# Halving the on-chip scratch of dynamic DMAs and giving the room to four more buffer slots

## The chip, the cores and the metric

The kernel runs on one core of a Trainium2 chip, as one program launched once. The metric is the device time of that launch in microseconds (us). The core has a matrix engine (TensorE, PE in the profile, with its weight loads shown as PEld), a vector engine (VectorE, DVE), a scalar engine (ScalarE, ACT), a general engine (GpSimd, POOL) and a queue engine that only issues transfers (SyncE, SP). Each works through its own queue of instructions in order, and they wait for each other by semaphores. TensorE's clock has two levels, 1.2 and 2.4 GHz; the profile gives the granted clock of a stretch as a share of the higher one.

## The reference, cut to what matters

Two transformer-like blocks of two layers each run one after the other on one sequence of 512 tokens with 1024 channels, in float32.

```python
def first_block(x, c, ...):
    h = layer_norm(x)
    for l in range(2):
        ada = (silu(c) @ w_ada[l] + b_ada[l])           # six modulation vectors
        u = h * (1.0 + sc1) + sh1
        y = mixer(u, ...)        # bidirectional mLSTM + dilated attention, gated, projected
        h = layer_norm(DN_ALPHA * h + g1 * y, ...)
        u = h * (1.0 + sc2) + sh2
        h = layer_norm(DN_ALPHA * h + g2 * swiglu(u, w1[l], w3[l], w2[l]), ...)
    return h

def second_block(x, c, ...):
    for layer in range(2):
        sh1, sc1, g1, sh2, sc2, g2 = adaln_params(c, ada_w[layer], ada_b[layer])
        h = rms_norm(x, ...) * (1.0 + sc1) + sh1
        if layer == 0:           # RG-LRU branch and stick-breaking attention
            mix = concat([lru(...) * gelu(gr), stick_breaking(q, k, v)]) @ ev_w_out
        else:                    # sliding-window attention with sinks
            mix = swa_sinks(q, k, v, sinks) @ od_w_out
        x = x + g1 * mix
        h = rms_norm(x, ...) * (1.0 + sc2) + sh2
        x = x + g2 * conv_ffn(h, ...)
    return x
```

Stick-breaking attention takes, per head and block of 128 queries, the scores `z`, `sp = softplus(z)` where the key is earlier than the query, the reversed running sum of `sp`, and the weights `exp(z - sum)`, which multiply the values.

## The kernel before, in words

Activations lie with channels on the 128 partitions and the 512 tokens along the row: a `[1024, 512]` array is eight tiles of 128 x 512 float32, 2048 bytes of a partition each. Every such tile, and every half of a high/low pair, is one **slot**. The pool has `NSLOT` of them (line 30). `Model.get` (line 561) takes the slot at the head of a queue `freeq`, and `Model.put` (line 566) hands slots back at its tail, so slots go round first in, first out; with F slots free, a `get` returns the slot that was handed back F `put`s earlier, and its first writer has to wait until the last reader of its former content is through. This is settled when the program is built. The framework then orders the instructions of each queue, sets the waits and lays out the memory: the scratch of the dynamic DMAs first, then constants, two buffers `wt` for raw weights, five pairs `wh`, `wl` for split weights, and the slots at the end.

Precision comes from splitting: a float32 value is a rounded part (high) and a remainder (low), and a projection sums three products. Weights arrive as one stream of 128 x 128 blocks, 16 to a transfer of 1 MB on SP's queue (line 596); for each eight of them ACT makes the high part (line 601) and DVE the low part (line 604). `proj` (lines 616 to 618) does three matmuls for each of the eight blocks into one of three `acc` banks of PSUM. PSUM further has two score banks `s` (pool `pss`), one bank `t` for transposes (`pst`) and two banks `o` (`pso`).

The stages, in order, with the lines that matter here:

- The start: `x` is loaded, normed (`Norm.plain`), and the first modulation is made tile by tile (`ada_tile`, line 830): four loads into slots (line 837, SP), matmuls (line 841), a copy (line 845), a transpose by matmul (line 848), a sum (line 850, DVE); then `u` (lines 1381 to 1383) and the first projections (lines 1388 to 1390).
- For each of two layers of the first block: four mLSTM heads, four attention pairs (`attention_pair`), gates and output projections (`mixer`), then the feed-forward (`ffn_first`). At the end of a pair POOL writes row sums to DRAM (line 1210) and reads them back spread over partitions with four DMAs (line 1214); DVE takes their difference (line 1218), ACT its tanh (line 1219). The next projections' gates are evacuated on ACT at line 1249. Inside a pair DVE writes the masked scores into a slot at line 1159, and the weighted values are summed by matmuls at lines 1189 and 1193.
- The joint between the blocks (`Chain`) norms twice at once, in two halves of 256 tokens: matmuls of squares and cross products (line 469), evacuations (line 487 on ACT, 488 on DVE), statistics, then the outputs tile by tile (lines 512 to 516, of which line 515 is on ACT). Line 665 is the first projection that reads them.
- The second block's first layer (`mix_even`, line 1608): the LRU, whose small weights come by DMAs on ACT's queue into a slot `bd` (line 1517), then four pairs of heads of stick-breaking attention (`stick_weights`, line 1567). For each pair the four query blocks run from the last to the first; the next pair's queries, keys and values (`heads`, with the head's norm at line 1447) are made after the first block. A step for one query block does for both heads: scores (lines 1487, 1488, 1576), two evacuations into slots `z` (line 1579) and `e` (line 1580), exponential and logarithm (1581, 1582), `sp` (1583), running sum (1584), difference (1586), exponential (1587), transposes (1590), evacuation (1591); then the weighted values (line 1604). `z` and `sp` go back after the transposes, `e` after the weighted values.
- The feed-forward, the sliding-window layer (`mix_odd`) and the last feed-forward.

Of the kernel before, what the change touches and what calls it, by code (L numbers as in the profile page):

```python
# [26 lines left out]
NBLK = 4176  # L27
CHUNK = 16
NCHUNK = NBLK // CHUNK
NSLOT = 57  # L30


FULL, HALF, MOVING = 0, 16, 112
# [493 lines left out]
class Model:  # L527
    def __init__(self, ctx, tc, ins, out, dbg=None, stop=None):
# [13 lines left out]
        self.slots = pool("slots", 1)  # L542
        self.freeq = deque(range(NSLOT))
        self.peak = NSLOT
        self.late = []
# [1307 lines left out]
```

## Time and profile before

| | us |
|---|---|
| median of 3 runs (3498.55 to 3499.63) | 3498.85 |
| the profiled execution's own time | 3499.55 |
| its span, first to last instruction | 3497.8 |
| PE busy in it | 3398.8 (97%) |
| DVE busy | 2158.0 (62%) |
| ACT busy | 1454.3 (42%) |
| POOL busy | 186.1 (5%) |
| mean granted clock of TensorE | 0.987 |

The profile records one execution. Busy time of an engine is the union of its instructions; the ends of matmuls are modelled, since they are pipelined. In a list of waits, "X L1 <- Y L2: a, n, b" says that engine X stood idle before its instruction of line 1 for a us in n waits, the longest b us, and that each ended when the instruction of line 2 on Y was done. In a timeline a line gives the start, the length, the engine, the line of the kernel, the operation, what it writes and reads, and in brackets the idle time of the engine before it and what ended that. A "q" behind an engine's name means its queue: a transfer that is issued there.

### The profile page before, as it was taken

How to read it: one execution, taken by the hardware profiler on the slowest of the kernel's cores; microseconds unless marked ns; L12 is line 12 of the kernel's file. 1: busy time of each engine (PE TensorE's matmuls, PEld its weight loads, DVE VectorE, ACT ScalarE, POOL GpSimd, SP SyncE). 2: the span in 40 equal slices, each digit the busy share in tenths (PEclk: the TensorE clock that was granted, in tenths of full speed). 3: DMA queues.
4: the chain of work that ended last, by engine and by line, in shares of the span. 5: the costliest groups of instructions: out<-in, count | busy, mean ns of one | idle time of the engine just before them, and what ended most of it. 6: DMA issues, size and time to landing. Idle time of an engine off the chain costs nothing.

```text
span 3497.8 us, 45346 instructions
## 1 busy us (share of the span) xinstructions
PE 3398.8 (97%) x17783; PEld 2791.3 (80%) x17783; DVE 2158.0 (62%) x4071; ACT 1454.3 (42%) x2536; POOL 186.1 (5%) x257
## 2 busy tenths in 40 slices
PE   7999998999999999999999999989999999999999
PEld 5888776878888888877688888877688888888887
DVE  5875544658664687555534856368788565875353
ACT  4543554224222554345423422237753233754231
POOL 1110011010000011001101000001000000000000
PEclk9999999999999999999999999999999999999999
DMA  5222222544552222222222546221136442113221
GB/s 217 91 79 79 84 73 79 206 156 164 187 209 103 76 88 79 91 73 73 86 90 85 186 176 210 99 70 61 37 108 220 162 148 86 60 61 109 96 97 73
DMA packets 76117, 395.72 MB, mean 113 GB/s; under 512 B 9200, under 2 KB 10480, under 8 KB 42496
## 3 DMA queue, kind: packets, MB, share of 16 engines
q1 hardware_dynamic: 69408, 377.90, 30.4%
q0 software_dynamic: 4480, 12.69, 1.2%
q8 instruction: 140, 2.29, 0.3%
q10 hardware_dynamic: 2016, 2.25, 0.2%
q14 instruction: 73, 0.60, 0.1%
HBM read 390.60 MB, written 2.20 MB: 112 GB/s over the span
## 4 chain that ended last, share of the span: by engine, by line
PE 44%; DVE 4%; ACT 1%; issue 1%; DMA 0%; DVEq 0%; ACTq 0%
PE acc L616 12%; PE acc L618 12%; PE acc L617 11%; PE acc L665 1%; PE acc L669 1%; PE acc L668 1%; PE o L1604 1%; PE t L1707 0%; DVE wl L604 0%; PE s L1487 0%; DVE slot L1584 0%; PE o L665 0%; PE o L668 0%; PE o L669 0%; PE s L1488 0%
## 5 line engine op out<-in xcount | busy, mean ns | idle before, releaser
L616 PE MATMUL acc<-slot,wh 128*128 128x512 f32 x3461 | 1368.5, 395 | 31.1 <-ACT slot L1249 14.3
L617 PE MATMUL acc<-slot,wh 128*128 128x512 f32 x3461 | 1363.1, 394 | 1.2 <-DVE slot L697 1.2
L618 PE MATMUL acc<-slot,wl 128*128 128x512 f32 x3461 | 1359.1, 393 | 0.0
L601 ACT CAST wh<-wt 128x1024 fp32r<-128x1024 f32 x522 | 547.7, 1050 | 1204.5 <-PE acc L617 1002.2
L604 DVE TENSOR_TENSOR wl<-wt,wh 128x1024 fp32r<-128x1024 f32 x522 | 645.5, 1238 | 512.3 <-ACT wh L601 504.0
L616 PEld LDWEIGHTS acc<-slot,wh 128*128 128x128 f32 x3461 | 654.1, 189 | 179.5 <-ACT slot L1249 15.1
L617 PEld LDWEIGHTS acc<-slot,wh 128*128 128x128 f32 x3461 | 653.9, 189 | 138.2 <-issue 6.0
L618 PEld LDWEIGHTS acc<-slot,wl 128*128 128x128 f32 x3461 | 653.3, 189 | 136.8 <-issue 5.0
L800 DVE SCALAR_TENSOR_TENSOR slot<-wada,csil,slot 128x512 f32<-128x512 f32 x308 | 231.8, 753 | 69.8 <-DMA wada<-in_ada_dram 64.1
L665 PE MATMUL acc<-slot,wh 128*128 128x256 f32 x726 | 206.9, 287 | 6.8 <-ACT slot L515 6.0
L668 PE MATMUL acc<-slot,wh 128*128 128x256 f32 x726 | 205.1, 283 | 0.0
L669 PE MATMUL acc<-slot,wl 128*128 128x256 f32 x726 | 204.1, 282 | 0.1
L696 ACT CAST slot<-slot 128x512 fp32r<-128x512 f32 x204 | 124.8, 619 | 174.6 <-POOL slot L1268 51.9
L1287 DVE SCALAR_TENSOR_TENSOR slot<-acc,ada,slot 128x512 f32<-128x512 f32 (+1 forms) x109 | 70.1, 646 | 155.4 <-PE acc L618 117.9
L895 DVE SCALAR_TENSOR_TENSOR slot<-acc,vecs,slot 128x510 f32<-128x510 f32 (+2 forms) x217 | 159.8, 745 | 7.6 <-ACT slot L890 4.9
L697 DVE TENSOR_TENSOR slot<-slot,slot 128x512 fp32r<-128x512 f32 x204 | 138.7, 688 | 24.6 <-ACT slot L696 22.9
L665 PEld LDWEIGHTS acc<-slot,wh 128*128 128x128 f32 x726 | 137.9, 191 | 14.2 <-ACT slot L515 6.6
L668 PEld LDWEIGHTS acc<-slot,wh 128*128 128x128 f32 x726 | 138.4, 191 | 2.0 <-issue 0.8
L669 PEld LDWEIGHTS acc<-slot,wl 128*128 128x128 f32 x726 | 137.7, 190 | 1.5 <-issue 0.8
L1159 DVE CUSTOM_DVE_ANT_0 slot<-s,slot 128x256 f32<-128x256 f32 (+1 forms) x128 | 48.2, 402 | 56.9 <-PE o L1193 31.4
L639 PE MATMUL acc<-wh,slot 128*128 128x256 f32 x288 | 82.1, 285 | 0.0
L642 PE MATMUL acc<-wh,slot 128*128 128x256 f32 x288 | 81.8, 284 | 0.0
(391 smaller groups left out, 3982.8 us busy)
## 6 DMA issues: line engine op xcount, KB each, us to landing
wt<-in_ws_dram SPq DMA_DIRECT2D x261, 1024.0 KB, 4.8
wada<-in_ada_dram SPq DMA_DIRECT2D x176, 512.0 KB, 4.5
slot<-in_ada_dram SPq DMA_DIRECT2D x32, 256.0 KB, 5.6
slot<-drc POOLq DMA_DIRECT2D x16, 256.0 KB, 3.7
slot<-in_bias_dram POOLq DMA_DIRECT2D x16, 256.0 KB, 2.9
slot<-dr POOLq DMA_DIRECT2D x32, 128.0 KB, 3.1
out_dram<-slot SPq DMA_DIRECT2D x8, 256.0 KB, 2.0
slot<-in_xT_dram SPq DMA_DIRECT2D x4, 256.0 KB, 5.3
```

The lines of the kernel that those rows point to most:

```text
L601: copy = nc.scalar.copy(self.wh, src)
L604: nc.vector.tensor_tensor(out=self.wl, in0=src, in1=self.wh, op=ALU.subtract)
L616: nc.tensor.matmul(acc, wh, xs[k].h.r, start=k == 0, stop=False)
L617: nc.tensor.matmul(acc, wh, xs[k].l.r, start=False, stop=False)
L618: nc.tensor.matmul(acc, wl, xs[k].h.r, start=False, stop=k == n - 1)
L665: m = nc.tensor.matmul(acc[:, hs], wh, xs[k].h.r[:, hs], start=k == 0, stop=False)
L668: nc.tensor.matmul(acc[:, hs], wh, xs[k].l.r[:, hs], start=False, stop=False)
L669: last[a] = nc.tensor.matmul(acc[:, hs], wl, xs[k].h.r[:, hs], start=False, stop=k == n - 1)
L696: copy = self.nc.scalar.copy(pair.h.r, src)
L697: self.nc.vector.tensor_tensor(out=pair.l.r, in0=src, in1=pair.h.f, op=ALU.subtract)
L800: nc.vector.scalar_tensor_tensor(out=acc.f, in0=wt[:, j, :], scalar=c, in1=acc.f, op0=ALU.mult, op1=ALU.add)
L895: nc.vector.scalar_tensor_tensor(out=out[:, lo:hi], in0=acc[:, lo + d:hi + d], scalar=w, in1=out[:, lo:hi], op0=ALU.mult, op1=ALU.add)
```

## The change

The scratch that the framework reserves at the start of each partition for dynamic DMAs (the descriptors of transfers that POOL issues) goes from its default of 16384 bytes to 8192. The 8192 bytes become four more slots of 2048 bytes: 61 instead of 57. Nothing else in the source changes.

```diff
-NSLOT = 57
+NSLOT = 61
@@
-    nc = bacc.Bacc("TRN2", target_bir_lowering=False, num_devices=1)
+    nc = bacc.Bacc("TRN2", target_bir_lowering=False, num_devices=1, dynamic_dma_scratch_size=8192)
```

## Rows read from the trace of the kernel before

**Rows 1.** The page: busy us, share of the span and instructions of each engine.
```profile
PE 3398.8 (97%) x17783; PEld 2791.3 (80%) x17783; DVE 2158.0 (62%) x4071; ACT 1454.3 (42%) x2536; POOL 186.1 (5%) x257
```

**Rows 2.** Windows: length, busy PE, PEld, DVE, ACT, POOL (instructions), clock, DMA share, GB/s.
```profile
2405.00:2510.00 105.00, 96.93 (x498) 72.24 (x497) 86.66 (x137) 76.72 (x151) 10.06 (x10) 0.97 0.17 61
2510.00:2560.00 50.00, 41.78 (x202) 29.05 (x201) 31.92 (x63) 31.33 (x75) 2.39 (x3) 0.83 0.00 1
3160.00:3210.00 50.00, 50.00 (x222) 41.40 (x222) 28.23 (x35) 19.25 (x25) 0.00 (x0) 1.00 0.26 89
350.00:600.00 250.00, 246.84 (x1279) 189.05 (x1279) 127.93 (x384) 127.66 (x288) 23.19 (x49) 1.00 0.22 76
```

**Rows 3.** Waits of ACT from 2510 to 2560 us, the end of stick-breaking.
```profile
ACT slot L1579 <- PE o L1604: 3.4, 4, 1.3
...
ACT slot L1579 <- PE t L1590: 1.3, 2, 0.7
ACT slot L1580 <- PE t L1590: 1.2, 1, 1.2
```

**Rows 4.** Waits of PE from 2510 to 2560 us.
```profile
PE t L1590 <- ACT slot L1587: 4.7, 3, 2.5
...
PE s L1487 <- ACT slot L1580: 1.0, 2, 0.5
```

**Rows 5.** The page: DMA issues, count, KB each, median us from issue to landing.
```profile
slot<-dr POOLq DMA_DIRECT2D x32, 128.0 KB, 3.1
```

**Rows 6.** Timeline after the first layer's last attention pair.
```profile
610.72 0.79 PE L616 MATMUL acc<-slot,wh 128*128 128x512 f32 x1 [8.71 <-ACT slot L1249]
```

**Rows 7.** Instructions of line 616: ns at least, median and most.
```profile
L616 PE MATMUL acc<-slot,wh x3461: 387/389/796, 93.7 to 3493.2; 128*128 128x512 f32 x193
```

**Rows 8.** Timeline of ACT at the end of stick-breaking.
```profile
2521.49 0.48 ACT L1579 ACTIVATE slot<-s,rq 128x256 f32<-128x256 f32 x1 [1.13 <-PE o L1604]
```

**Rows 9.** Waits of PE from 2400 to 2570 us.
```profile
PE s L1447 <- ACT slot L1445: 3.8, 1, 3.8
```

**Rows 10.** Timelines of PE, ACT and DVE in the second half of `Chain`.
```profile
2330.26 0.62 PE L469 MATMUL s<-slot,slot 128*32 128x256 f32 x2
...
2330.07 0.34 ACTq L1517 DMA_DIRECT2D slot<-in_wa_dram  x1
2330.45 0.91 ACT L515 ACTIVATE slot<-slot,ada 128x256 fp32r<-128x256 f32 x2 [3.65 <-PE o L665]
...
2331.27 0.35 ACT L487 COPY slot<-s 128x256 f32<-128x256 f32 x1
...
2330.99 0.88 DVE L516 SCALAR_TENSOR_TENSOR slot<-slot,ada,slot 128x256 fp32r<-128x256 f32 x2 [5.32 <-ACT slot L515]
...
2341.15 0.62 PE L665 MATMUL acc<-slot,wh 128*128 128x256 f32 x3 [3.02 <-ACT slot L515]
```

**Rows 11.** Waits of SP's queue in the first 140 us.
```profile
SPq L837 <- DVE slot L1383: 5.8, 1, 5.8
SPq L837 <- DVE slot L879: 5.0, 1, 5.0
```

**Rows 12.** Windows of 4 us at the start, columns as in rows 2.
```profile
28.00:32.00 4.00, 2.67 (x28) 1.60 (x28) 3.93 (x6) 1.59 (x3) 2.27 (x2) 1.00 0.58 181
32.00:36.00 4.00, 1.43 (x5) 0.86 (x5) 4.00 (x4) 1.07 (x2) 3.21 (x2) 0.93 0.58 171
36.00:40.00 4.00, 2.46 (x8) 2.17 (x9) 3.97 (x7) 2.48 (x3) 1.98 (x2) 0.50 0.17 29
```

**Rows 13.** Timeline of PE at the start.
```profile
29.81 1.07 PE L841 MATMUL s<-slot,csil 128*32 128x256 f32 x16
```

**Rows 14.** Waits of DVE from 350 to 600 us, the first layer's attention.
```profile
DVE slot L1159 <- PE o L1193: 15.9, 10, 2.0
```

**Rows 15.** Waits of all engines, and of PE's weight loads, over the span.
```profile
ACT wh L601 <- PE acc L617: 1002.2, 331, 6.7
...
PEld acc L616 <- ACT wh L601: 11.3, 8, 4.1
```

## The prediction, written before the result was known

> **What bounds the kernel now.** I read the engines' busy shares first. PE is busy 3398.8 us of the 3497.8 us span, DVE 62%, ACT 42%, and POOL, the engine whose DMAs use the scratch that is halved, 5% [rows 1]. So PE sets the time, and a change that takes no work from PE can win only where PE stands still or runs at a lower granted clock: 3497.8 - 3398.8 = 99.0 us idle. Next I cut the span into windows. A stretch of feed-forward matmuls has PE busy 50.00 of 50.00 us at clock 1.00 [rows 2]; slots can give nothing there. The stick-breaking attention is different: of its last 50 us PE is busy 41.78, at a granted clock of 0.83 [rows 2].
>
> Then I asked which idle time hangs on a slot. A wait for a slot shows as a wait for an instruction that is no input of the waiting one, but the last reader of what lay in the slot before. L1579 and L1580 read only the score bank and `rq`; yet ACT waits there for L1604 (the matmul that used up an older `es`) and for L1590 (the transpose that read an older `ss`): 3.4 + 1.3 + 1.2 = 5.9 us in the last 50 us of the stage [rows 3]. PE, in the same stretch, waits 4.7 us for L1587 and 1.0 us for L1580, the end and the start of that same chain [rows 4].
>
> The code says why. Slots go round in a first-in first-out queue, so a `get` receives the slot handed back as many `put`s ago as there are free slots. In pair 2 of `mix_even`, with the next pair's heads made, 8 (`x`) + 16 (`u`) + 8 (`ya`) + 4 (`yb`) + 1 (`strict`) + 1 (kept by the norm) + 2 x 7 (two pairs' `qa`, `ka`, `vn`) = 52 are held and 5 are free. One step takes 6. Its second head must reuse the `z` of its first, and the next step's second head the `es` of the step before, which L1604 has just read. With 9 free, a step's six gets need nothing of its own, and a step waits only for the L1604 two steps back.
>
> **The change part by part.** *The scratch.* It lies at the start of each partition, ahead of all tiles; it removes and adds no instruction. POOL's DMAs come two to four together, and a broadcast of `dr` lands 3.1 us after its issue [rows 5]. I cost it at nothing, covered by the pauses between these groups. Bounds: below nothing is excluded, since a smaller scratch makes no descriptor sooner; above, if each of the four L1214 issues of a pair had to wait for the landing of the one before, 3 x 3.1 = 9.3 us, and that has no cover after the last pair of a layer, where PE already stands 8.71 us behind this hand-over [rows 6]: 2 layers x 9.3 = 19 us. The Trainium skill (DMA: Bandwidth & Descriptors, The descriptor swizzle; its Terms give 16 B for a descriptor) counts 9 descriptors on an engine for a 128-partition transfer; by that page I estimate 8192 / (9 x 16) = 56 such DMAs at once in the smaller ring, and the bound of 19 us would be 0. No run here shows it.
>
> *Addresses.* Every tile moves down by 8192 bytes, the slots too. The 3461 matmuls of L616 read slots all over the pool, and last 387 ns at the least and 389 in the median [rows 7]: where a slot lies makes no difference, so 0 on both sides.
>
> *Four more slots, stick-breaking, last 50 us.* Here no projection is left to fill PE. Of the 5.9 us of ACT's slot waits [rows 3] I take half, 3.0 us, as reaching PE: one of them starts the chain at 2521.49 [rows 8] and another stands before a stretch in which PE has its own work. Bounds 0 (the next wait comes as late) and 8.2 (all of the idle time, 50.00 - 41.78). The lower clock: 41.78 us of busy time at 0.83 would be 41.78 x 0.83 = 34.7 at full clock, so 7.1 us are lost; the drop comes with the idle time, so I take it in the same share, 3.0 / 8.2 x 7.1 = 2.6 us; bounds 0 and 7.1. What is late next: the score bank, of which there are two (PE waits for L1580 [rows 4]), and the one `t` bank.
>
> *The 105 us before.* PE idles 105.00 - 96.93 = 8.1 us at DVE 83% busy [rows 2]; 3.8 us of it is one wait for the first head's key, at L1447, which no slot delays [rows 9], and projections of the next pair cover most slot waits. I take 1.0 us; bounds 0 and 8.1 - 3.8 = 4.3.
>
> *Into the second block (`Chain`).* When the first half's `u` is made, 8 + 3 + 1 + 1 + 2 + 22 (`gs`) + 4 + 16 = 57 slots are held: none is free. ACT's queue holds the DMA of `bd` (L1517), whose slot is one that a matmul of L469 still reads; it is issued at 2330.07, and L515 behind it only then starts, after 3.65 us of idle ACT; DVE, which waits for L515, is idle 5.32 us; so the evacuation L487, needed by the second half's mean, starts at 2331.27, some 0.4 us after L469's last end (2330.26 + 0.62), with 0.91 us of late L515 ahead of it, and PE later stands 3.02 us [rows 10]. With slots handed back four `put`s earlier this DMA need not wait. I take 1.5 us (L487 about 0.4 earlier, and DVE without a backlog); bounds 0 and 3.0.
>
> *The start.* SP holds the `ada0` loads (L837) 5.8 us for L1383 and 5.0 us for L879 [rows 11]: counting through the queue, the loads of tiles 5 to 7 land in slots of the norm and of tiles 0 and 1's `t`. With four more they get slots whose readers are done by 24 us. Meanwhile PE is busy 2.67, 1.43 and 2.46 of 4 us [rows 12], and 16 matmuls of a tile take 1.07 us [rows 13]; two tiles fit into the hole before the score bank and DVE's L850 hold the next: at most 2.1 us, at least 0 where the order of PE's queue stays. I take 0.5.
>
> *Attention and mLSTM.* DVE waits 15.9 us for slots at L1159 in the first layer's attention [rows 14], but PE is busy 246.84 of 250 us there [rows 2]: the next pair's projections cover it. 0; bounds 0 and 3.2, the idle time.
>
> Sum: 3.0 + 2.6 + 1.0 + 1.5 + 0.5 = 8.6 us. Against the profiled execution's own 3499.55 us (span 3497.8 and 1.75 around it) that is 3490.95; the median of the runs is 0.70 below that execution, so I say 3490.
>
> **The rivals.** *Hidden, no change (3497).* The banks take over as the last wait: there are two score banks and one `t` bank, and PE's wait for L1580 [rows 4] is one of these already. Then only the terms outside the stage stay, 2 us. For it: the chain within a step (L1579 to L1591) is untouched. Against: the slot waits on ACT are longer than this bank wait.
>
> *A larger gain (3475).* Waits also hide under PE's busy time. The Trainium skill (Perfetto Trace Analysis, Identifying the Most-Contended Engine) says that matmul busy share is no measure of the distance to the roofline and that weight loads are. The rows agree as far as they go: weight loads fill 41.40 of 50.00 us in the feed-forward stretch but 189.05 of 250 in the attention, where PE counts as 99% busy [rows 2]. At the former's density those loads need 189.05 x 50.00 / 41.40 = 228.3 us: 21.7 us of slack a layer. If the 15.9 us at L1159 came off at half their size in both layers, 2 x 8 = 16 us more, and the rest from the terms above: 3499 - 8 - 16, about 3475. Against: the small matmuls there have costs of their own, and the projections still have to be done.
>
> *Slower, by a new order (3508).* The framework orders each queue when the program is built, and what it puts first depends on when a slot comes free. If ACT and DVE work that slots held back now goes ahead of the casts L601 and L604, PE gets its weights later. The price: about 0.6 us of ACT a time, and PE's weight loads already wait 11.3 us in 8 places for L601 [rows 15]; if 15 operations that come free hit such a place, 15 x 0.6 = 9 us more, without the gain, about 3508. It decides from where fewer than one cast is in hand. Against: in 331 places ACT waits for PE to free a cast buffer, 1002.2 us in all [rows 15]; the casts are mostly far ahead.
>
> *The scratch throttles POOL* (above): 19 us less the gain, 3509.
>
> **How the numbers follow.** Forecast (3490): 0.40. Hidden: 0.22. Larger gain: 0.16. New order: 0.19. Scratch: 0.03. 0.2%, about what a measurement of this kernel can tell from no change, is 7 us: 3491.9 to 3505.8. The forecast's own spread, 3483 to 3497 from its bounds, puts 0.26 of its 0.40 below 3491.9; with the larger gain that is 0.42 faster. Hidden (0.22), the rest of the forecast (0.14) and 0.04 of the new order stay within: 0.40. The rest of the new order and the scratch are slower: 0.18. The range leaves out half of the larger gain and a quarter of the slower cases: 3474 to 3509; the forecast's own range is 3483 to 3497.
>
> **What would show it.** Right: in the last 50 us of the stick-breaking stage, ACT's waits for L1604 and L1590 under 2 us, PE busy share up, clock above 0.83; no idle ACT before L515 in `Chain`; SP's waits at L837 for L879 and L1383 gone. Hidden: these waits gone, PE's idle time there the same, its waits now for L1580 or L1591. New order: more waits of PE's loads for L601 or L604. Scratch: L1214 longer than 0.5 us, `dr` landing later. The prediction is wrong if the idle sum of 99 us moves elsewhere, in places that no slot wait marked before.

## The result, and the profile after

The changed kernel takes 3457.82 us (median; 3455.43 to 3459.48) against 3498.7 for the kernel before (with a fourth run of it); the ratio is 0.9887, with a 95% interval of 0.987 to 0.9904. It is 41 us faster: the sign was right, and the size was not. The forecast was 3490, and the time lies below the lower end of the range, 3474.

The first view is the page's row of busy times and the row of the core's span and mean granted clock, of the changed kernel:

```profile
PE 3377.9 (98%) x17783; PEld 2781.7 (81%) x17783; DVE 2154.6 (62%) x4071; ACT 1448.3 (42%) x2536; POOL 190.9 (6%) x257
...
core 0: 3453.6 us, clock 0.993
```

Beside [rows 1]: the span is 44.2 us shorter in these two executions. PE's idle time fell from 99.0 to 3453.6 - 3377.9 = 75.7 us, which is 23.3 us. The other 20.9 us came off PE's *busy* time, though it has the same 17783 matmuls. The clock accounts for that: by the mean clocks, which are rounded to 0.001, an estimated 3398.8 x 0.987 = 3354.6 us of work at full clock before, and 3377.9 x 0.993 = 3354.3 after. So in this pair of executions about half of the gain is idle time and half is work that no longer runs at the lower clock. Over all executions on record the mean granted clock is 0.9882 for the kernel before (54 of them) and 0.9928 for the changed one (8); on some 3390 us of busy time that makes an estimated 15.5 of the 41 us. The Trainium skill (Perfetto Trace Analysis, Identifying the Most-Contended Engine) warns that matmul busy time is no good measure of how close a kernel is to roofline, because pipelined instructions look smaller in a trace. These two rows agree, for another reason: 20.9 us of busy time vanished with no matmul gone.

Where did it go? The next view gives, for a line, its instructions: shortest, median and longest ns, and the start of the first and of the last. The kernel before:

```profile
L1153 PE MATMUL s<-slot,slot x128: 377/379/483, 351.9 to 1723.4; 128*128 128x256 f32 x128
...
L932 PE MATMUL t<-consts,slot x16: 221/223/273, 88.5 to 1222.4; 64*128 64x64 f32 x16
...
L469 PE MATMUL s<-slot,slot x32: 379/379/403, 2299.9 to 2330.5; 128*32 128x256 f32 x32
...
L1519 PE MATMUL s<-slot,slot x16: 590/592/592, 2366.1 to 2389.0; 128*128 128x512 f32 x16
...
L1576 PE MATMUL s<-slot,ident_r x32: 276/281/562, 2422.6 to 2550.8; 128*128 128x256 f32 x32
...
L1590 PE MATMUL t<-consts,slot x80: 270/273/476, 2431.2 to 2556.7; 128*128 128x128 f32 x80
```

The changed kernel:

```profile
L1153 PE MATMUL s<-slot,slot x128: 377/379/382, 352.2 to 1698.7; 128*128 128x256 f32 x128
...
L932 PE MATMUL t<-consts,slot x16: 221/223/273, 88.8 to 1208.5; 64*128 64x64 f32 x16
...
L469 PE MATMUL s<-slot,slot x32: 379/379/403, 2273.2 to 2301.9; 128*32 128x256 f32 x32
...
L1519 PE MATMUL s<-slot,slot x16: 590/592/592, 2336.0 to 2359.0; 128*128 128x512 f32 x16
...
L1576 PE MATMUL s<-slot,ident_r x32: 277/281/387, 2391.8 to 2506.0; 128*128 128x256 f32 x32
...
L1590 PE MATMUL t<-consts,slot x80: 270/273/330, 2400.4 to 2513.5; 128*128 128x128 f32 x80
```

The differences of the starts, in the order of the program: the first score of the first layer's attention (L1153, first) +0.3 us; the last of L932, in the second layer's mLSTM, -13.9; the first L469, in `Chain`, -26.7; the first LRU matmul (L1519) -30.1; the first stick-breaking score (L1576) -30.8; its last transposes (L1590) -43.2; the end of the program -44.2. So the stretch that holds the first layer's attention (with its gates and the feed-forward behind them) gave 14.2 us, that of the second 12.8, the joint 3.4, stick-breaking 12.4, all the rest 1.4. The forecast had put the first two at nothing.

Three things that the prediction named can be ticked off in rows of the changed kernel. The scratch: POOL's L1214 takes 526 ns, and `dr` lands after 2.9 us, not 3.1 [rows 5]. The prediction's sign, an L1214 of more than 0.5 us, could tell nothing: it took 523 ns in the median, and 516 at the least, before the change too.

```profile
L1214 POOL DMA_DIRECT2D slot<-dr x32: 518/526/544, 381.7 to 1717.0; - x32
...
slot<-dr POOLq DMA_DIRECT2D x32, 128.0 KB, 2.9
```

`Chain`, in timelines of ACT and PE: the DMA of `bd` is issued while ACT is still busy, L487 follows L469 with nothing of L515 ahead of it, and PE's later wait is 2.11 us instead of 3.02 [rows 10].

```profile
2297.19 0.33 ACTq L1517 DMA_DIRECT2D slot<-in_wa_dram  x1
2302.78 0.37 ACT L487 COPY slot<-s 128x256 f32<-128x256 f32 x1 [5.20 <-PE o L469]
...
2312.33 1.01 PE L665 MATMUL acc<-slot,wh 128*128 128x256 f32 x3 [2.11 <-ACT slot L515]
```

From the first L469 to the first L1519, 362 matmuls in both (windows, columns as in [rows 2]; first before, then after), PE idles 10.3 us, then 9.0, and its mean clock rises from 0.87 to 0.92:

```profile
2300.00:2366.00 66.00, 55.71 (x362) 46.37 (x358) 54.21 (x112) 28.17 (x53) 0.00 (x0) 0.87 0.21 72
```

```profile
2273.30:2336.00 62.70, 53.70 (x362) 45.04 (x361) 53.03 (x111) 27.76 (x52) 0.00 (x0) 0.92 0.22 76
```

The start: SP's waits for L1383 and L879 [rows 11] are gone from its list, and PE is no busier than before in windows of 4 us (1.43 and 2.46 us in [rows 12]):

```profile
32.00:36.00 4.00, 1.45 (x5) 0.86 (x5) 4.00 (x4) 1.07 (x2) 3.40 (x3) 0.95 0.38 142
36.00:40.00 4.00, 2.26 (x7) 2.02 (x8) 3.96 (x7) 2.28 (x3) 1.78 (x2) 0.50 0.00 0
```

### The profile page after: what moved, and what is told of

It reads as the page before. It is cut to its first block, busy times and chain, and to the rows that moved or that the text cites. A ratio compares the mean times of both kernels' runs of the same rounds, so it can differ in the third digit from the quotient of the medians.

```text
span 3453.6 us, 45259 instructions
## 1 busy us (share of the span) xinstructions
PE 3377.9 (98%) x17783; PEld 2781.7 (81%) x17783; DVE 2154.6 (62%) x4071; ACT 1448.3 (42%) x2536; POOL 190.9 (6%) x257
## 4 chain that ended last, share of the span: by engine, by line
PE 87%; DVE 7%; ACT 2%; DMA 2%; issue 1%; POOL 0%; SPq 0%; ACTq 0%; DVEq 0%; POOLq 0%
PE acc L616 22%; PE acc L617 22%; PE acc L618 22%; PE acc L665 2%; PE acc L668 2%; PE acc L669 2%; PE o L1604 1%; PE o L1189 1%; PE s L1153 1%; PE acc L639 1%; PE acc L643 1%; PE acc L642 1%; DMA wada<-in_ada_dram 1%; PE o L1193 1%; DVE wl L604 1%
## 5 line engine op out<-in xcount | busy, mean ns | idle before, releaser
L616 PE MATMUL acc<-slot,wh 128*128 128x512 f32 x3461 | 1365.5, 395 | 16.4 <-DVE slot L895 10.3
L601 ACT CAST wh<-wt 128x1024 fp32r<-128x1024 f32 x522 | 547.9, 1051 | 1241.9 <-PE acc L617 1023.5
L616 PEld LDWEIGHTS acc<-slot,wh 128*128 128x128 f32 x3461 | 651.9, 188 | 162.8 <-ACT wh L601 10.9
L800 DVE SCALAR_TENSOR_TENSOR slot<-wada,csil,slot 128x512 f32<-128x512 f32 x308 | 231.9, 753 | 63.7 <-DMA wada<-in_ada_dram 57.9
L643 PE MATMUL acc<-wl,slot 128*128 128x256 f32 x288 | 81.5, 283 | 0.0
```

What stands on the lines that cost most here:

```text
L601: copy = nc.scalar.copy(self.wh, src)
L616: nc.tensor.matmul(acc, wh, xs[k].h.r, start=k == 0, stop=False)
L800: nc.vector.scalar_tensor_tensor(out=acc.f, in0=wt[:, j, :], scalar=c, in1=acc.f, op0=ALU.mult, op1=ALU.add)
```

## What was tried, and what each run showed

The two traces leave open what the attention had gained, and whether four slots, a smaller scratch, or merely another order of the instructions did it. Times are medians; each ratio is to runs of the kernel before on the same chip (3496.8 to 3500.2 us). Where an edit adds lines, the lines behind it have higher numbers in its rows.

### The scratch alone

```diff
-NSLOT = 61
+NSLOT = 57
```

> The scratch is halved to 8192 bytes, and the slots stay at 57: all tiles move down, no order changes. Theory of the slots (the 41 us come from four more slots alone): 3498.7 us, within 2, and every stage as long as before. Rival, scratch or addresses take part in the gain: below 3490. Rival, the smaller scratch costs something that the slots more than repaid: above 3503, with L1214 longer than 0.5 us or rows of dr landing later than 3.1 us.

Measured: 3496.74 us, ratio 0.9998 (0.9988 to 1.0008). The order of the instructions is that of the kernel before. Neither the scratch nor the 8192 bytes by which all tiles moved count. The Trainium skill (DMA: Bandwidth & Descriptors, The descriptor swizzle) counts nine read and nine write descriptors on an engine for a 128-partition transfer of 1 MiB. The estimate made from it, room for some 56 transfers in the smaller ring, takes one of the two sides; were both in the same room, it would be 28. This run is consistent with either and tests neither: POOL's transfers come two to four together.

### Slots lent to a part of the program

In these kernels 57 slots go round, and the other four are put into `freeq` at one place; at another, the four that then stand at its head are taken out. No instruction is added.

```diff
-        self.freeq = deque(range(NSLOT))
+        self.freeq = deque(range(57))
+        self.spare = [57, 58, 59, 60]
+    def lend(self):
+        self.freeq.extend(self.spare)
+    def take_back(self):
+        self.spare = [self.freeq.popleft() for _ in range(4)]
```

From the first attention pair to the last gate of each layer:

```diff
+        self.lend()
         ob = [self.attention_pair(l, sp, u) for sp in range(4)]
...
         self.put(obp, u)
+        self.take_back()
```

> Scratch 8192, 57 slots; the four more are in the queue only from the first attention pair to the last gate of a layer, in both layers of the first block, and are taken out again. Theory of two places (the end of the attention gives about 27 us, the end of stick-breaking about 14): 3498.7 - 27 = 3472, the 8.71 us of idle PE after the first layer's last pair gone, clock there 1.00; stick-breaking as before (clock 0.83 in its last 50 us). Rival, the gain belongs to a new order of the whole program that any change of the queue of slots may or may not bring: a time anywhere, 3458 or 3499, with idle PE in other places than before.

Measured: 3469.86 us, ratio 0.9913 (0.9897 to 0.993), 27.5 us faster.

From the start of stick-breaking to its end:

```diff
         self.ln_exp_table(sq)
+        self.lend()
...
         self.put(u, self.strict)
+        self.take_back()
```

> Scratch 8192, 57 slots; the four more are in the queue only from the start of stick-breaking in the second block to its end. Theory of two places: 3498.7 - 16 = 3483 (13.6 us of it in the last 50 us, where the clock no longer falls, and 2.6 us in the 105 us before); the holes of 8.71 and 5.57 us after the attention stay. Rival, banks are the last wait there and the gain of the full change in this stage came from an earlier order: 3497.

Measured: 3484.91 us, ratio 0.9957 (0.9942 to 0.9972), 12.4 us faster. The two together are 39.9 of the 41 us, each known to within some 6 us. The gain is made in two places, by slots, and adds up; it is not a new order of the whole program that happened to be better. The traces bear this out: of PE's 17783 matmuls, all but a few stand in the order of the kernel before outside the two attention stretches (350 to 600 and 1450 to 1750 us) in the first of these kernels, and outside stick-breaking in the second.

### Why the attention gained: the gate on ACT

In the kernel before, the hole of 8.71 us [rows 6] ends when ACT's L1249 frees a bank. That instruction stands on ACT behind L1219, the tanh of the last pair, which waits for `dr`. In the changed kernel the first L1249 stands ahead of it. My first theory was that this alone had filled the hole. The test puts it back:

```diff
-        nc.scalar.activation(d.f, d.f, AF.Tanh, scale=0.5)
+        self.tanh = nc.scalar.activation(d.f, d.f, AF.Tanh, scale=0.5)
...
-            nc.scalar.activation(th.f, acc, AF.Tanh, scale=0.5)
+            gate = nc.scalar.activation(th.f, acc, AF.Tanh, scale=0.5)
+            if m == 0:
+                self.behind(gate, self.tanh)
```

> All as in the changed kernel, 61 slots, but ACT's evacuation of the first gate after the attention (L1249) is ordered behind the tanh of the last pair (L1219), where it stood before the change. Theory (the hole of 8.71 us is the first gate stuck on ACT behind the tanh that waits for dr's way through DRAM, since its slot was one that the last pair's difference had read): a hole of some 6 to 9 us is back in each layer, with the low clock behind it, 3457.8 + 2 x 10 = about 3478. Rival, the gain in the attention is spread over the waits at L1159 and the gate only changed its place: within 5 us of 3457.8.

Measured: 3455.62 us, ratio 0.987 (0.9856 to 0.9885), as fast as the changed kernel. The theory fell. The rows show why. First the kernel before: the transpose that ends the first layer's last pair (L1206), a window from there to the hole, and one that holds the hole (columns as in [rows 2]).

```profile
596.61 0.28 PE L1206 MATMUL t<-consts,att_l 128*16 128x128 f32 x1
...
596.60:602.03 5.43, 4.81 (x20) 3.23 (x19) 3.51 (x5) 2.46 (x5) 2.18 (x5) 1.00 0.14 26
...
602.00:620.00 18.00, 9.29 (x32) 7.46 (x32) 9.44 (x13) 4.92 (x6) 1.68 (x2) 0.72 0.45 150
```

Then the kernel with the gate behind the tanh: the same transpose and the window to PE's next idle time, of 1.31 us, which ends with DVE's L800 and not with `dr`.

```profile
586.44 0.28 PE L1206 MATMUL t<-consts,att_l 128*16 128x128 f32 x1
...
586.43:598.63 12.20, 11.64 (x50) 8.95 (x49) 10.30 (x15) 5.33 (x8) 3.55 (x6) 1.00 0.60 189
```

DVE's L1218 is the first to use what `dr` brought; in the kernel before, and with the gate behind:

```profile
607.17 1.02 DVE L1218 TENSOR_TENSOR slot<-slot,slot 128x512 f32<-128x512 f32 x1 [3.04 <-DMA slot<-dr]
```

```profile
596.44 1.09 DVE L1218 TENSOR_TENSOR slot<-slot,slot 128x512 f32<-128x512 f32 x1 [0.30 <-DMA slot<-dr]
```

The way of `dr` through DRAM is about as long in both: from L1206 to L1218 it is 607.17 - 596.61 = 10.6 us, and 596.44 - 586.44 = 10.0. (In the kernel before ACT then loads a table for 1.28 us ahead of the tanh, from 608.26; with the gate behind, that load is over before L1218.) What differs is what PE has left to do in it. While `dr` is under way, and the first gate stands behind the tanh, only the first three projections of the gates can run, one for each `acc` bank: 3 x 24 = 72 matmuls. Before, the first window has 20 instructions, 18 of them such matmuls (the others are L1206 and a matmul still running): 54 of the 72 had been used up *inside* the last pair. With 61 slots the window has 50, 48 of them such matmuls; only 24 were used up earlier, and the pair ends 10.2 us sooner. The last pair alone, from its first score to L1206, with DVE's wait for a slot in it; before, and with the gate behind:

```profile
562.90:596.70 33.80, 33.09 (x189) 23.10 (x187) 19.95 (x78) 20.13 (x54) 0.00 (x0) 1.00 0.09 32
...
DVE slot L1159 <- PE o L1193: 4.5, 3, 2.0
```

```profile
560.50:586.50 26.00, 25.22 (x157) 17.56 (x156) 18.69 (x78) 20.09 (x55) 0.00 (x0) 1.00 0.12 42
...
DVE slot L1159 <- PE o L1193: 4.0, 2, 2.3
```

It is 7.8 us shorter, and the 30 matmuls fewer, at 0.23 us from one to the next, are an estimated 6.8 of these; the rest of the 10.2 us is an earlier start. Over all four pairs DVE's slot wait at L1159 falls from 15.9 us [rows 14] to this:

```profile
DVE slot L1159 <- PE o L1193: 5.7, 3, 2.3
```

But in the last pair it is nearly what it was. So this wait is not what shortened that pair, and what made the framework put 54 matmuls into it instead of 24 stays open. What the runs show is the result: with more slots the last pair uses up less of the matmuls that PE then needs behind it. PE was busy beside the pair's waits, so their cost stood as idle time only where those matmuls ran out. The lower clock after the hole is part of the bill: in the window that holds it 9.29 us are busy at a mean clock of 0.72, which is an estimated 6.7 at full clock, 2.6 less.

### The same cover, spent or kept

If that is so, the matmuls can hide either the pair's waits or the way of `dr`, and without more slots nothing is won by choosing. In a kernel with 57 slots (and a scratch of 8192) the first four projections, three of which have a bank, are held back on PE until the last pair is over:

```diff
-        nc.tensor.transpose(t[0:16, 0:P], ls, self.ident)
+        self.ending = nc.tensor.transpose(t[0:16, 0:P], ls, self.ident)
...
             acc = self.proj("w_in", l, BR0 + m * P, u)
+            if m < 2:
+                self.behind(self.first, self.ending)
...
             acc = self.proj("w_a", l, m * P, hmp)
+            if m < 2:
+                self.behind(self.first, self.ending)
```

(`self.first` is the first matmul of a projection.)

> 57 slots, scratch 8192; the first three projections of the gates are ordered behind the transpose that ends the last pair (L1206) on PE, so they can't fill the waits inside that pair. Theory (cover is spent once: it hides the pair's slot waits or the way of dr, not both): the holes of 8.71 and 5.57 us are gone, PE stands idle 8 to 12 us inside the last pair of each layer instead, and the time is the same within 6 us, 3491 to 3503. Rival, only the order was bad, and the slots are not needed for the gain: 3475 to 3485.

Measured: 3494.05 us, ratio 0.9988 (0.9979 to 0.9997). Windows of the last pair (with its longest wait) and of the stretch behind it, this kernel, and below it the last pair of the kernel before:

```profile
565.00:596.00 31.00, 23.66 (x131) 15.97 (x129) 18.82 (x77) 19.41 (x54) 0.00 (x0) 0.82 0.11 35
...
590.80 0.41 PE L1173 MATMUL t<-consts,slot 128*128 128x128 f32 x2 [1.73 <-DVE slot L1066]
...
596.00:612.00 16.00, 16.00 (x67) 13.16 (x67) 8.48 (x12) 5.28 (x7) 3.85 (x6) 0.92 0.11 34
```

```profile
565.00:596.00 31.00, 30.31 (x172) 21.02 (x171) 18.75 (x74) 18.08 (x51) 0.00 (x0) 1.00 0.10 35
```

The hole is gone, 16.00 of 16.00 us busy, and 31.00 - 23.66 = 7.3 us of idle time stand inside the pair, at clock 0.82, where there were 0.7. The time is almost that of the kernel before. The cover was moved, not made.

More slots help in two ways, and the next three runs part them. Lent to the four pairs alone, taken out before the gates:

```diff
+        self.lend()
         ob = [self.attention_pair(l, sp, u) for sp in range(4)]
+        self.take_back()
```

> 57 slots; the four more are lent to the four attention pairs of each layer and taken out before the first gate, which then gets a slot that the last pair's difference read, and stands behind the tanh on ACT, as in the kernel before. Theory of spent cover (with more slots a pair ends some 10 us earlier, so that the matmuls of the gates, which before went to fill its waits, are left for the way of dr through DRAM): all of the 27 us, 3470 to 3473, some 48 projection matmuls between the last L1206 of a layer and the next idle PE, against 18 and 15 before. Rival, the gate's own slot made the hole: holes of 5 us or more stay, 3485 to 3495.

Measured: 3478.68 us, ratio 0.995 (0.9933 to 0.9967), 18.9 us faster. The window from L1206 has 40 instructions, 38 of them projections, and a hole of 3.34 us stays, which the expectation had not:

```profile
586.94:595.97 9.03, 9.02 (x40) 6.99 (x39) 4.45 (x6) 2.55 (x5) 2.59 (x5) 1.00 0.23 68
...
599.29 0.79 PE L626 MATMUL acc<-slot,wh 128*128 128x512 f32 x1 [3.34 <-ACT slot L1261]
```

Lent to the last pair of each layer alone:

```diff
+            if sp == 3:
+                self.lend()
+            ob.append(self.attention_pair(l, sp, u))
+        self.take_back()
```

> As lend_pairs, but the four slots are lent to the last pair of each layer only. Theory of spent cover: only the last pair has a hole behind it, the others hand what they save to projections that have to be done anyway, so most of the gain stays: 3474 to 3482. Rival, what is saved adds up over the pairs: a quarter to a half of the 27 us, 3485 to 3492.

Measured: 3482.7 us, ratio 0.9958 (0.9941 to 0.9975), 14.9 us faster: four fifths of what all four pairs gave, just outside what the theory expected (3474 to 3482) and outside the rival (3485 to 3492). The hole that stays is the same 3.34 us. The pairs before the last hand on little: the 4.0 us between the two runs are less than their intervals can tell apart.

Lent to the gates alone, at the head of the queue:

```diff
+        self.freeq.extendleft(self.spare)
         for m in range(8):
...
         self.put(obp, u)
+        self.take_back()
```

> 57 slots through the attention; the four more are put at the head of the queue for the gates only, so that the first four gates need no slot of the last pair, and stand ahead of the tanh on ACT. Theory that the attention must end earlier: its last pair ends as late as before, its cover is spent, and the hole only gets smaller: 3485 to 3495. Rival, the gate's slot made the hole, and more matmuls may now run while dr is under way: 3470 to 3478.

Measured: 3476.29 us, ratio 0.9939 (0.9924 to 0.9954), 21.2 us faster, against the expectation. The pair ends late (PE's L1216, which is L1206, starts at 598.93), and still there is no hole. ACT's first gate (L1260 in this kernel) and the window behind the pair:

```profile
580.27 0.60 ACT L1260 ACTIVATE slot<-acc 128x512 f32<-128x512 f32 x1
...
598.90:615.00 16.10, 16.10 (x73) 13.34 (x73) 10.95 (x15) 6.84 (x10) 4.11 (x6) 1.00 0.40 133
```

The first gate has its slot at 580.27, inside the pair, and frees its bank, so a fourth projection can start: more cover. Either remedy, slots in the pairs (18.9) or more work to put beside their waits (21.2), fills most of the same hole. Together (`lend_attention`) they gave 27.5, not 40.

### Stick-breaking

The changed kernel, the last 36.5 us of the stage: window, ACT's slot waits, and PE's waits.

```profile
2480.00:2516.50 36.50, 33.33 (x192) 22.95 (x191) 28.24 (x57) 24.78 (x63) 1.78 (x2) 1.00 0.01 1
...
ACT slot L1579 <- PE o L1604: 1.5, 1, 1.5
ACT slot L1579 <- PE t L1590: 0.2, 1, 0.2
...
PE o L1604 <- DVE slot L1591: 1.5, 2, 0.8
PE s L1487 <- ACT slot L1580: 0.3, 1, 0.3
```

ACT's waits for L1604 and L1590, 5.9 us before [rows 3], are 1.7. PE idles 36.50 - 33.33 = 3.2 us, and the clock stays at its higher level. This window holds 192 matmuls and that of [rows 2] 202, so their busy times are not of the same work. Windows of 721 matmuls each, before and after, are:

```profile
2400.00:2560.00 160.00, 143.72 (x721) 105.31 (x720) 123.58 (x205) 110.82 (x230) 14.06 (x14) 0.93 0.11 40
```

```profile
2370.00:2516.50 146.50, 135.92 (x721) 99.51 (x720) 121.58 (x205) 108.40 (x230) 13.67 (x14) 0.99 0.12 44
```

In these PE idles 10.6 us instead of 16.3, which is 5.7 less, and is busy 7.8 us less. The fourth pair of heads alone, from its first score to its last values, before and after:

```profile
2526.58:2558.20 31.62, 26.90 (x125) 18.43 (x123) 20.26 (x42) 19.94 (x49) 0.00 (x0) 0.73 0.00 1
```

```profile
2488.18:2514.70 26.52, 25.16 (x146) 17.24 (x144) 19.63 (x42) 18.28 (x47) 0.00 (x0) 1.00 0.00 1
```

It is 5.1 us shorter and holds 21 more instructions of PE. Again they are mostly, 17 of them, matmuls kept for it: L683 to L685, the next output projection, 96 in all in this stage. Ahead of the fourth pair's first score, L683 had run 18 times before, 13 times after (all three lines together 54 before, 37 after):

```profile
2498.40:2526.58 28.18, 7.34 (x18) 3.21 (x17) 1.00 0.00 1
```

```profile
2470.60:2488.18 17.58, 5.20 (x13) 2.34 (x13) 1.00 0.17 61
```

Is it the fourth pair's own slots, or what the earlier pairs leave it? Two runs lend the four slots to one or to the other.

```diff
+            if pr == 3:
+                self.lend()
             o = self.pso.tile([P, T], F32, name="o")
```

> 57 slots; the four more are lent to the last of the four pairs of heads of stick-breaking only. Theory (the gain of 12 us there sits where no projection of a next pair is left, and is mostly the clock, which no longer falls): 3487, clock 1.00 in the last 35 us of the stage. Rival, the earlier pairs bring the work ahead by which the last one keeps PE busy: 3493 or more, clock under 0.9 there.

Measured: 3495.82 us, ratio 0.9995 (0.9985 to 1.0005): nothing. The 18 matmuls of this line (here L693) are spent as before, and the clock falls:

```profile
2490.00:2525.04 35.04, 7.35 (x18) 3.39 (x18) 1.00 0.09 31
...
2512.00:2550.00 38.00, 30.39 (x151) 21.09 (x149) 26.53 (x50) 25.36 (x64) 0.00 (x0) 0.82 0.00 1
```

The other way round, in the queue for the first three pairs and out before the fourth (`take_back` in the place of `lend` above):

> 57 slots; the four more are lent to the first three pairs of heads of stick-breaking and taken out before the last. Theory of spent cover (the earlier pairs no longer use up the matmuls of the next output projection, L683 to L685, so the last pair finds them): 3485 to 3489, some 37 of the 96 done before the last pair's first score, as in the changed kernel, against 54 before. Rival, the last pair needs the slots itself, and both have to come together: 3492 or more.

Measured: 3489.13 us, ratio 0.9968 (0.9954 to 0.9982), 10.5 us faster. 13 matmuls of the line are spent, as after the change, and the clock is at 0.92:

```profile
2490.00:2517.44 27.44, 5.20 (x13) 2.44 (x13) 1.00 0.11 40
...
2507.00:2549.00 42.00, 37.39 (x196) 26.16 (x195) 30.49 (x58) 26.96 (x66) 3.84 (x4) 0.92 0.00 1
```

So most of the gain is made in the three pairs that PE's busy share called covered, and is paid out in the fourth. With the slots in all four (`lend_stick`) the clock holds to the end:

```profile
2510.00:2546.50 36.50, 33.68 (x197) 24.03 (x197) 27.77 (x58) 25.05 (x62) 0.00 (x0) 1.00 0.00 1
```

### How many slots

Only `NSLOT` and, for 62 and 63 slots and one run with 61, the scratch are changed:

```diff
-NSLOT = 61
+NSLOT = 63
...
-dynamic_dma_scratch_size=8192
+dynamic_dma_scratch_size=4096
```

> 58 slots, scratch 8192. Theory of spent cover (each slot takes off a part of the waits, and the hole is what the cover then misses): about half of the way, 3470 to 3485, holes after the attention of 2 to 5 us, 37 instead of 54 matmuls of the gates spent inside the last pair, clock in the last 40 us of stick-breaking still under 1.00. Rival, two slots at once are needed: 3492 or more. Rival, one slot is enough: 3463 or less.

> 59 slots, scratch 8192. Theory (each slot more takes off a part of the slot waits, and the cover lasts longer by as much): about half of the gain, 3472 to 3484, holes after the attention of 2 to 5 us. Rival, a threshold (a step needs all four): 3492 or more. Rival, the order of the program is chance: slower than 3500, or as fast as 61.

> 60 slots, scratch 8192. Theory of spent cover (a gain ends where the cover lasts; with 59 slots the hole after the attention is gone already): the same as 59 and 61, 3453 to 3463. Rival, the order of the program is chance: more than 6 us away from both, on either side.

> The changed kernel itself once more, on the same chip as the three others: 3458, as on record, within 4.

> 62 slots, scratch 4096. Theory of spent cover (what 63 gained it gained in stretches where something was still left, the mLSTM and the end of the first attention): between 61 and 63, 3446 to 3458. Rival, chance of the order: above 3461 or under 3443.

> 63 slots, scratch 4096. Theory (the cover now lasts to the end of both stages, what idle time is left there is no slot's): within 6 us of the 61 slots, 3451 to 3462. Rival, the gain goes on by 10 us a slot: under 3445. Rival, a scratch of 4096 holds up POOL's transfers: over 3465, with L1214 longer than 0.6 us.

> 61 slots, scratch 4096: the changed kernel with a quarter of the scratch. If 63's further gain is its slots: the same as 61 with 8192, 3455 to 3461. If it is the scratch or the addresses: 3444 to 3449.

| slots | scratch, bytes | us | ratio (95%) |
|---|---|---|---|
| 57 | 8192 | 3496.74 | 0.9998 (0.9988 to 1.0008) |
| 58 | 8192 | 3476.59 | 0.9939 (0.9922 to 0.9956) |
| 59 | 8192 | 3458.35 | 0.9881 (0.9866 to 0.9895) |
| 60 | 8192 | 3460.58 | 0.9883 (0.9869 to 0.9898) |
| 61 | 8192 | 3454.88 | 0.9873 (0.9858 to 0.9887) |
| 61 | 4096 | 3457.20 | 0.9876 (0.9862 to 0.9891) |
| 62 | 4096 | 3449.10 | 0.9852 (0.9835 to 0.9868) |
| 63 | 4096 | 3446.29 | 0.9847 (0.9832 to 0.9862) |

The first slot gives half and the second the other half; the third and fourth give nothing that these runs can tell; the fifth and sixth some 9 to 11 us together. 61 slots with a scratch of 4096 are no faster than with 8192, so that last step is the slots' too. Neither "half with 59" nor "nothing more after 61" was right: 59 slots are as fast as 61, which is what the rival that calls the order chance allowed; 60 and 62 slots then lay where the theory of spent cover put them. With 58 slots no hole stands behind the attention; the order that the framework found keeps the cover and leaves the idle time inside the last pair instead, the other choice of the run above (PE's largest wait there, at 583.27, is 2.46 us).

63 slots beat both kernels. What the last two slots fill was not traced to a single place, and 59 to 61 slots differ stage by stage though their sums agree; how much of that is the order that the framework happens to find stays open.

## Why the prediction was wrong

- *What bounds the kernel.* "A change ... can win only where PE stands still or runs at a lower granted clock: 99.0 us idle" was sound as a frame (23.3 us and 20.9 us), but the second half was then priced in one window only.
- *Attention and mLSTM: 0.* This step failed, and carries some 27 of the 41 us (27.5 in `lend_attention`). "The next pair's projections cover it" holds for the first three pairs, as far as `lend_last` can tell. The fourth has no next pair: its cover is the three projections of the gates, the same that PE needs while `dr` is under way. The cover was counted as free, and the hole behind it [rows 6] as a fixed price of `dr`; the bounds, 0 and 3.2 us, were the idle time inside the stretch, and left out the hole that the stretch makes.
- *Stick-breaking, 3.0 + 2.6 + 1.0 us.* The signs were right: the waits named fell to 1.7 us, and idle time and clock changed as said. The terms were mis-sized: 5.7 us of idle time against 4.0, 7.8 of busy time against 2.6, 12.4 from the first score to the last transposes. Taking the clock in the share of the idle time was the wrong scale, since with 3.2 us of idle time left it did not fall at all. The premise "no projection is left to fill PE" was wrong: in the fourth pair 30 matmuls of the next output projection still ran before the change, and 47 after it. And the place was half wrong. The count of 5 free slots is that of the third pair; by the same count the fourth, which has no next heads, holds 47 and had 10 free all along. Slots for it alone brought nothing, and slots in the first three pairs alone 10.5 us, where I had 1.0.
- *`Chain`, 1.5 us.* The order changed as said, and 3.4 was measured, just above its bound of 3.0: 1.3 of it is idle time (0.9 PE's wait for L515), and the rest busy time at a higher clock, which the term left out. No run tests this stage alone.
- *The start, 0.5 us.* SP's waits went, PE gained nothing (+0.3 us): the lower bound.
- *Scratch and addresses, 0.* Right.
- *Rivals.* "A larger gain" was right that time hides under a busy PE in the attention. Its sum for that, 16 us for both layers, was too small against some 27, its wait (L1159) hardly fell in the pair that matters, and its mechanism was another, slack of the weight loads; the runs show spent cover instead. It also left the stick-breaking term as it was. "Hidden" is refuted: the banks did not take over. "A new order" is refuted as a loss: PE's loads wait 10.9 us for L601, against 11.3 [rows 15].

## What to carry to other kernels

A stall hidden under other work is not free while that work is limited: ask which instructions hide it, how many there are until the next thing that needs them, and whether a hole stands where they run out. Here what too few slots cost beside a PE that was 99% busy was paid where the stage ends, as a hole of 8.71 us with a low clock behind it. And when few buffers go round, count the idle time *behind* a stage as part of what one more buffer may bring.

## What the hardware did that was not expected

The granted clock fell beside small pauses too: in the last 31 us of the attention without cover, idle times of at most 1.73 us, 7.3 in all, went with a clock of 0.82, while the changed kernel's last 36.5 us of stick-breaking, with 3.2 us in pauses of at most 0.82, ran at 1.00. In the two profiled executions the change of the clock accounts for 20.9 us, nearly as much as the 23.3 us of idle time. A scratch of 4096 bytes, a quarter of the default, cost POOL's transfers nothing that can be measured: `dr` landed after 2.9 us with 61 slots and 3.0 with 63.
